# A transformer block on one core: a fifth Strassen pair, the odd gate product moved ahead of a change of pools, tiles shifted by 32 bytes

## The chip, the cores and the metric

The kernel runs on one NeuronCore of a Trainium2 chip. The metric is device time in microseconds (us) of one execution. TensorE (PE) multiplies matrices; VectorE (DVE) and ScalarE (ACT) work element by element; GpSimd (POOL) hardly works here; SyncE (SP) starts the DMAs. TensorE's stationary operand is loaded by a separate instruction, shown as PEld.

## The reference

One block on a sequence of 256 rows of 2048 numbers, float32:

```python
xn = rms_norm(h, norm1_g)
proj = xn @ w_in                        # u, v | q | c_kv | index q, k, w | gates
y_a = u * (W_s @ layer_norm(v) + b)     # chunk-causal spatial gating, gelu on u, v
y_b = sparse_attention(q, c_kv, ...)    # the top 64 keys of each query, by an indexer
mixed = g_a * (y_a @ w_oa) + g_b * (y_b @ w_ob)
h = h + mixed @ w_out
hn = rms_norm(h, norm2_g)
h = h + (silu(hn @ w_gate) * (hn @ w_up)) @ w_down      # w_gate, w_up: 2048 x 5632
out = rms_norm(h, final_g)
```

## The kernel before

Nearly all weights pass through the chip once. Each float32 operand is split in two, a high part rounded to float32r by ACT and the low rest by DVE (`split`, L70 to L78), and a product takes three matmuls: high by high, high by low, low by high (`mm3`, L88). The 256 rows make two tiles of 128, the 2048 columns four blocks of 512.

**Projections** (up to L494). Weights come in chunks of 128 x 1024 through the pool `wp` with four buffers each for the raw weights, their high and their low part (`wchunk`, L80). A natural group (`nat_group`, L93) has slices of x stationary and 512 weight columns moving. A transposed group (`tr_group`, L108; index queries, queries and keys) has 128 weight columns stationary and the 256 rows of x moving. The first projection (`kv`, L228 to L241) reads its chunk in two column halves of 296. The last of these stages is the output projection (L473), four blocks n; behind each come the residual add (L478), transposes on PE, and the operand for the feed-forward part. The feed-forward operand has 16 tiles of k, in eight pairs j. For j below `NS`, `s_operand` (L160) makes eight combinations of the pair's four 128 x 128 quarters for a Strassen product; for the others the tiles are only split.

**Feed-forward** (from L497). `pre.close()` gives up the pools of the projections, and `wq` and `fp` are laid over their bytes; a new tile waits for the old ones beneath it. A weight quad is 128 x 4 x 512, 1 MB, through three buffers (`quad`, `quad_split`). Eleven column blocks of 512 form five pairs, done by `s_group` (L520), and an odd one (`LB`), done by `plain_group`. An `s_group` makes 256 x 1024 of the gate or the up product. It goes over eight pairs j in `ORDER`. A Strassen pair (j below NS) takes DVE's three sums of weight quarters into `sums` (L534 to L536), a split of three raw quarters (1536 wide) and one of the four sums (2048 wide), and 7 products. A plain pair takes one split of 2048 and 8 products. The four Strassen sums m1, m5, m6, m7 lie in one PSUM pool of four banks (`aux`), the four results in the other (`acc`). After the last Strassen pair DVE combines the four into `u` (L549 to L553), after the last pair it evicts the results (L566 to L571).

PE's order is that of the program from L626 on (`manual_schedule`); the other engines' and everything before is ordered by Tile's scheduler. The order is: odd gate product, gate group 0, odd up product, up group 0, the odd block's down products, then for i = 1 to 4 gate group i, two down products of the pair before, up group i, two more. Beside the last half pair of a gate group PE transposes the block before for its down products (`beside`, L557); these transposes take `aux` banks.

Of the kernel before, what the change touches and what calls it, by code (L numbers as in the profile page):

```python
# [16 lines left out]
P = 128  # L17
# [13 lines left out]
KVW = LAT + IDXD + IDXH  # L31
NEG = -1.0e38
MARK = -3.0e38
NS = 4

A12, A22, A11, S1, S3, S2, S4, A21 = range(8)
WARM = 8
# [3 lines left out]
def block_kernel(ctx: ExitStack, tc: tile.TileContext, a, out):  # L41
# [4 lines left out]

    nc = tc.nc
    const = ctx.enter_context(tc.tile_pool(name="const", bufs=1))
    tp = ctx.enter_context(tc.tile_pool(name="tp", bufs=20))
    acc_p = ctx.enter_context(tc.tile_pool(name="acc", bufs=4, space=bass.MemoryType.PSUM))  # L50
    aux_p = ctx.enter_context(tc.tile_pool(name="aux", bufs=4, space=bass.MemoryType.PSUM))
    pre = ExitStack()
    np_ = pre.enter_context(tc.tile_pool(name="np", bufs=11))
    tq = pre.enter_context(tc.tile_pool(name="tq", bufs=4))
    wp = pre.enter_context(tc.tile_pool(name="wp", bufs=4))
    sp = pre.enter_context(tc.tile_pool(name="sp", bufs=1))
# [1 line left out]
    def t_tile(name, dt=F32R):  # L58
        return tp.tile([P, 4, T], dt, tag="T", name=name)
# [7 lines left out]
    def aux_tile(name):  # L67
        return aux_p.tile([P, 512], F32, tag="aux", name=name)
# [8 lines left out]
            nc.scalar.activation(h, src, AF.Copy, scale=scale)  # L77
            nc.vector.scalar_tensor_tensor(l, src, scale, hf, op0=ALU.mult, op1=ALU.subtract)  # L78

    def wchunk(src, cols):  # L80
        raw = wp.tile([P, 1024], F32, tag="raw", name="raw")
        h = wp.tile([P, 1024], F32R, tag="wh", name="wh")
        l = wp.tile([P, 1024], F32R, tag="wl", name="wl")
        nc.sync.dma_start(raw[:, :cols], src)
        split(h[:, :cols], l[:, :cols], raw[:, :cols])
        return h, l
# [21 lines left out]
    def tr_group(w, ks, x, name, bank=acc_tile, beside=None):  # L108


        acc = [bank(f"{name}_{b}").rearrange("p (c t) -> p c t", c=2) for b in range(2)]
        for c in range(len(ks) // 2):
            wh, wl = wchunk(w[c], 1024)
            for j in range(2):
                i = 2 * c + j
                xh, xl = x(ks[i])
                for ct in range(4):
                    s = slice(j * 512 + ct * P, j * 512 + (ct + 1) * P)
                    o = acc[ct // 2][:, ct % 2, :]
                    last = i == len(ks) - 1  # L120
                    nc.tensor.matmul(o, wh[:, s], xh, start=(i == 0 and ct % 2 == 0), stop=False,  # L121
                                     skip_group_check=True)
                    nc.tensor.matmul(o, wh[:, s], xl, start=False, stop=False, skip_group_check=True)  # L123
                    nc.tensor.matmul(o, wl[:, s], xh, start=False, stop=last, skip_group_check=True)  # L124
            if beside is not None:
                beside(c)
        return acc
# [345 lines left out]
    for n in range(4):  # L473
        hx = tp.tile([P, 2, 512], F32, tag="T", name=f"h{n}")
        nc.sync.dma_start(hx, x_nat[n])
        acc = nat_group(a["w_out"][n], KS, of(mx_t), f"out{n}")
        for t in range(2):
            nc.vector.tensor_tensor(hx[:, t], acc[t], hx[:, t], op=ALU.add)  # L478
        if 2 * n >= NS:
            h, l = t_tile(f"hh{n}"), t_tile(f"hl{n}")  # L480
            transposed(hx, f"h{n}", h, l, scale=g2[:, 4 * n:4 * n + 4])
            hT += [(z[0][:, s], z[1][:, s]) for z, s in (((h, l), slice(0, 2)), ((h, l), slice(2, 4)))]
        else:
            for b in range(2):
                k = 4 * n + 2 * b
                pt = aux_tile(f"h{n}_pt{b}").rearrange("p (c t) -> p c t", c=2)
                for c in range(2):
                    for t in range(2):
                        ct = 2 * b + c
                        nc.tensor.transpose(pt[:, c, t * P:(t + 1) * P], hx[:, t, ct * P:(ct + 1) * P], ident)  # L490
                hT.append(s_operand(pt, f"hS{k}", g2[:, k:k + 2]))
        sumsq(ss2, hx, n)
        hn.append(hx)
    r2 = row_rstd(ss2, "r2")  # L494


    pre.close()  # L497
    wq = ctx.enter_context(tc.tile_pool(name="wq", bufs=3, reuse_waits="tile"))
    fp = ctx.enter_context(tc.tile_pool(name="fp", bufs=1, reuse_waits="tile"))
# [11 lines left out]
        split(h, l, raw)  # L511
        return h, l

    def h_tile(k, t):

        return tuple(z[:, k % 2, t * P:(t + 1) * P] for z in hT[k // 2])

    ORDER = (0, 4, 1, 5, 2, 3, 6, 7)

    def s_group(w, name, beside=None):  # L520

        m1, m5, m7, m6 = (aux_tile(f"{name}_{z}") for z in ("m1", "m5", "m7", "m6"))
        c11, c12, c21, c22 = (acc_tile(f"{name}_{z}") for z in ("c11", "c12", "c21", "c22"))
        u = fp.tile([P, 4, 512], F32, tag="u", name=f"{name}_u")
        for n, j in enumerate(ORDER):
            first = n == 0
            if j < NS:  # L530
                raw = quad(w[j])
                tt = wq.tile([P, 4, 512], F32, tag="sums", name="sums", bufs=1)

                nc.vector.tensor_tensor(tt[:, 0:2], raw[:, 1:3], raw[:, 0:1].to_broadcast([P, 2, 512]), op=ALU.add)  # L534
                nc.vector.tensor_tensor(tt[:, 2], tt[:, 0], raw[:, 2], op=ALU.add)
                nc.vector.tensor_tensor(tt[:, 3], tt[:, 2], raw[:, 3], op=ALU.add)  # L536
                wh, wl = quad_split(raw[:, 1:4], 3)
                th, tl = quad_split(tt)
                xh, xl = hT[j]
                todo = [(m1, A11, wh, wl, 0), (c12, S4, wh, wl, 1), (c11, A12, wh, wl, 2),  # L540
                        (m5, S1, th, tl, 0), (m7, S3, th, tl, 1), (m6, S2, th, tl, 2), (c21, A22, th, tl, 3)]
                if first:
                    todo = [todo[z] for z in (0, 3, 4, 5, 6, 1, 2)]
                for o, s, h, l, i in todo:
                    mm3(o, xh[:, s], xl[:, s], h[:, i], l[:, i], first, j == NS - 1 and o in (m1, m5, m6, m7))
                if j == NS - 1:


                    nc.scalar.activation(u[:, 0], m1, AF.Copy)  # L549
                    nc.vector.tensor_tensor(u[:, 2], m6, u[:, 0], op=ALU.add)  # L550
                    nc.vector.tensor_tensor(u[:, 1], m7, u[:, 2], op=ALU.add)
                    nc.vector.tensor_tensor(u[:, 2], m5, u[:, 2], op=ALU.add)
                    nc.vector.tensor_tensor(u[:, 3], m5, u[:, 1], op=ALU.add)  # L553
            else:
                wh, wl = quad_split(quad(w[j]))
                for c in range(2):
                    if j == ORDER[-1] and c == 1 and beside is not None:  # L557
                        beside()
                    for t, i, o in ((0, 1, c11), (1, 1, c21), (0, 0, c12), (1, 0, c22)):

                        i = (i if c == 0 else (2, 3)[i])
                        xh, xl = h_tile(2 * j + c, t)
                        mm3(o, xh, xl, wh[:, i], wl[:, i], o is c22 and j == ORDER[1] and c == 0,
                            j == ORDER[-1] and c == 1)

        def f(t, j, dst=None):  # L566
            dst = u[:, 2 * j + t] if dst is None else dst
            if j == 0:
                nc.vector.tensor_tensor(dst, (c11, c21)[t], u[:, t], op=ALU.add)
            else:  # L570
                nc.vector.tensor_tensor(dst, (c12, c22)[t], u[:, 2 + t], op=ALU.subtract)  # L571
        return f, u
# [18 lines left out]
        at[b] = (h, l)  # L591

    def gate_blocks(i, beside):
        f, _ = s_group(a["w_fg"][i], f"fg{i}", beside)
        s = [f_tile(f"s{i}_{j}") for j in range(2)]
        for j in range(2):
            for t in range(2):
                f(t, j, s[j][:, t])
                nc.scalar.activation(s[j][:, t], s[j][:, t], AF.Silu, scale=r2[:, t:t + 1])
        return s  # L600
# [16 lines left out]
            nc.vector.scalar_tensor_tensor(hn[n][:, t], acc[t], r2[:, t:t + 1], hn[n][:, t],  # L617
                                           op0=ALU.mult, op1=ALU.add)

    def plain_x(k, t):  # L620
        if k < 2 * NS:
            return tuple(z[:, (A11, A12, A21, A22)[2 * t + k % 2]] for z in hT[k // 2])
        return h_tile(k, t)

    order = ctx.enter_context(ExitStack())
    order.enter_context(tc.manual_schedule(engines={mybir.EngineType.PE}))  # L626

    LB = NFB - 1

    def odd_gate():  # L630
        acc = plain_group([a["w_fg10"][c] for c in range(4)], plain_x, KT, f"fg{LB}")
        s = f_tile(f"s{LB}")
        for t in range(2):
            nc.scalar.activation(s[:, t], acc[t], AF.Silu, scale=r2[:, t:t + 1])
        return s

    def odd_up(s):
        acc = plain_group([a["w_fu10"][c] for c in range(4)], plain_x, KT, f"fu{LB}", aux_tile)
        for t in range(2):
            nc.vector.tensor_tensor(s[:, t], acc[t], s[:, t], op=ALU.mult)  # L640

    odd = odd_gate()
    for i in range(LB // 2):
        if i == 0:
            s = gate_blocks(0, None)
# [79 lines left out]
def _layout(np, i):  # L725
# [14 lines left out]
    def quads(w):  # L740
# [24 lines left out]
        "w_out": chunks(np.asarray(i["w_out"])[0]),  # L765
        "w_fg": strassen(np.asarray(i["w_ff_gate"])[0][:, :FF - 512]),
        "w_fu": strassen(np.asarray(i["w_ff_up"])[0][:, :FF - 512]),
        "w_fg10": quads(np.asarray(i["w_ff_gate"])[0][:, FF - 512:])[0],
        "w_fu10": quads(np.asarray(i["w_ff_up"])[0][:, FF - 512:])[0],
        "w_fd": quads(np.asarray(i["w_ff_down"])[0]),  # L770
        "final_g": np.asarray(i["final_g"]).reshape(2, 2, 512),
# [19 lines left out]
```

## Time and profile before

| | us |
|---|---|
| median of 3 runs (1607.43 to 1608.71) | 1608.19 |
| the profiled execution | 1608.13 |
| its span, first to last instruction | 1606.3 |
| PE busy | 1587.4, 99% |
| DVE busy | 1103.8, 69% |
| ACT busy | 778.1, 48% |
| 16 DMA queues' share | 55%, 191 GB/s |

A busy PE is one with a matmul in flight; matmuls overlap, so the pace is read from their starts. A wait is put down to what ended it. The chain that ended last is followed back from the last instruction.

### The profile page before, as it was taken

To read this page: it belongs to the slowest core of one execution; us is meant where nothing else is said; L and a number is where in the kernel's file an instruction comes from. 1 tells how busy PE (TensorE), PEld (TensorE's weight loads), DVE (VectorE), ACT (ScalarE), POOL (GpSimd) and SP (SyncE) were. 2 spreads that over 40 slices of the span, in tenths; PEclk is the share of its full clock that TensorE was granted. 3 is DMA by queue.
4 is the path that set the end of the run, shared out by engine and by line. 5 is a ranking of instruction groups with operands and counts; after the bars stand their busy time and mean duration, and the time that the engine had idled before them with its cause. 6 is when DMAs were issued, how large, how long until landed. Compare 5 with 4: busy or idle time off the path is not lost.

```text
span 1606.3 us, 19668 instructions
## 1 busy us (share of the span) xinstructions
PE 1587.4 (99%) x7834; PEld 1337.8 (83%) x7834; DVE 1103.8 (69%) x1216; ACT 778.1 (48%) x815; POOL 1.6 (0%) x8
## 2 busy tenths in 40 slices
PE   9999999999999999999999899999999999999997
PEld 8988989889778888888888688878888888888886
DVE  5695655565754444555564787888789778888785
ACT  6554454554544444444453654455445445446442
POOL 0000000000000000000000000000000000000000
PEclk9999999999999999999999999999999999999999
DMA  9646555545545555555665454555545555555561
GB/s 310 213 136 198 193 173 171 175 167 184 175 149 193 190 195 195 187 194 185 205 202 209 184 207 185 188 208 207 200 175 213 197 184 202 217 184 223 190 242 53
DMA packets 69115, 307.48 MB, mean 191 GB/s; under 512 B 8160, under 2 KB 8416, under 8 KB 52128
## 3 DMA queue, kind: packets, MB, share of 16 engines
q1 hardware_dynamic: 69024, 306.24, 55.3%
q8 instruction: 61, 1.00, 0.2%
q14 instruction: 30, 0.25, 0.0%
HBM read 304.11 MB, written 2.10 MB: 191 GB/s over the span
## 4 chain that ended last, share of the span: by engine, by line
PE 93%; DVE 4%; ACT 2%; issue 0%; DMA 0%; SPq 0%; ACTq 0%; DVEq 0%
PE fd L90 4%; PE fd L89 4%; PE fd L91 4%; PE g L89 4%; PE g L91 4%; PE g L90 4%; PE fu_c L90 3%; PE fu_c L91 3%; PE fu_c L89 3%; DVE wl L75 2%; PE fg_c L91 2%; PE fg_c L89 2%; PE fg_c L90 2%; PE q L124 2%; PE q L121 2%; PE q L123 2%
## 5 line engine op out<-in xcount | busy, mean ns | idle before, releaser
L75 DVE TENSOR_TENSOR wl<-raw,wh 128x1024 fp32r<-128x1024 f32 (+3 forms) x434 | 639.5, 1477 | 364.9 <-ACT wh L74 364.0
L74 ACT ACTIVATE wh<-raw 128x1024 fp32r<-128x1024 f32 (+3 forms) x434 | 545.4, 1262 | 541.7 <-PE g L91 86.0
L74 ACT ACTIVATE wh<-sums 128x2048 fp32r<-128x2048 f32 x40 | 76.7, 1917 | 172.5 <-DVE sums L536 141.4
L75 DVE TENSOR_TENSOR wl<-sums,wh 128x2048 fp32r<-128x2048 f32 x40 | 91.7, 2293 | 68.3 <-ACT wh L74 68.2
L89 PE MATMUL fd<-wh,ah 128*128 128x512 f32 x320 | 124.6, 389 | 0.0
L91 PE MATMUL fd<-wh,al 128*128 128x512 f32 x320 | 124.5, 389 | 0.0
L90 PE MATMUL fd<-wl,ah 128*128 128x512 f32 x320 | 124.5, 389 | 0.0
L91 PE MATMUL g<-wh,xl 128*128 128x512 f32 x256 | 100.9, 394 | 0.0
L89 PE MATMUL g<-wh,xh 128*128 128x512 f32 x256 | 100.8, 394 | 0.0
L90 PE MATMUL g<-wl,xh 128*128 128x512 f32 x256 | 99.9, 390 | 0.0
L124 PE MATMUL q<-xh,wl 128*128 128x256 f32 x256 | 72.5, 283 | 0.0
L121 PE MATMUL q<-xh,wh 128*128 128x256 f32 x256 | 72.5, 283 | 0.0
L123 PE MATMUL q<-xl,wh 128*128 128x256 f32 x256 | 72.4, 283 | 0.0
L89 PEld LDWEIGHTS fd<-wh,ah 128*128 128x128 f32 x320 | 60.1, 188 | 12.5
L91 PEld LDWEIGHTS fd<-wh,al 128*128 128x128 f32 x320 | 60.1, 188 | 12.5
L90 PEld LDWEIGHTS fd<-wl,ah 128*128 128x128 f32 x320 | 60.1, 188 | 12.4
L89 PE MATMUL fg_c<-wh,hh 128*128 128x512 f32 x160 | 62.6, 391 | 0.0
L89 PE MATMUL fu_c<-wh,hh 128*128 128x512 f32 x160 | 62.3, 390 | 0.0
L91 PE MATMUL fg_c<-wh,hl 128*128 128x512 f32 x160 | 62.3, 389 | 0.0
L90 PE MATMUL fg_c<-wl,hh 128*128 128x512 f32 x160 | 62.3, 389 | 0.0
L91 PE MATMUL fu_c<-wh,hl 128*128 128x512 f32 x160 | 62.2, 389 | 0.0
L90 PE MATMUL fu_c<-wl,hh 128*128 128x512 f32 x160 | 62.2, 389 | 0.0
(303 smaller groups left out, 3420.1 us busy)
## 6 DMA issues: line engine op xcount, KB each, us to landing
raw<-in_w_fg SPq DMA_DIRECT2D x44, 1024.0 KB, 4.8
raw<-in_w_fu SPq DMA_DIRECT2D x44, 1024.0 KB, 4.8
raw<-in_w_fd SPq DMA_DIRECT2D x44, 1024.0 KB, 4.7
raw<-in_w_z SPq DMA_DIRECT2D x64, 512.0 KB, 3.3
raw<-in_w_g SPq DMA_DIRECT2D x64, 512.0 KB, 3.2
raw<-in_w_q SPq DMA_DIRECT2D x32, 512.0 KB, 3.3
raw<-in_w_oa SPq DMA_DIRECT2D x32, 512.0 KB, 3.3
raw<-in_w_ob SPq DMA_DIRECT2D x32, 512.0 KB, 3.3
```

Source lines behind the costliest of these rows:

```text
L74: nc.scalar.activation(h, src, AF.Copy)
L75: nc.vector.tensor_tensor(l, src, hf, op=ALU.subtract)
L89: nc.tensor.matmul(o, lh, rh, start=start, stop=False, **kw)
L90: nc.tensor.matmul(o, lh, rl, start=False, stop=False, **kw)
L91: nc.tensor.matmul(o, ll, rh, start=False, stop=stop, **kw)
L121: nc.tensor.matmul(o, wh[:, s], xh, start=(i == 0 and ct % 2 == 0), stop=False, skip_group_check=True)
L123: nc.tensor.matmul(o, wh[:, s], xl, start=False, stop=False, skip_group_check=True)
L124: nc.tensor.matmul(o, wl[:, s], xh, start=False, stop=last, skip_group_check=True)
```

## The change

- `NS` goes from 4 to 5: pair 4, too, is a Strassen pair, in five gate and five up groups. `ORDER` becomes 0, 5, 1, 2, 6, 3, 4, 7. The output projection's block 2 now makes one Strassen operand and one plain pair, so that both kinds are made in one loop.
- The odd block's gate product leaves the feed-forward's manual order. It stands before `pre.close()`, with 1024-wide chunks through `wchunk` (eight of 512 KB instead of four of 1 MB), and `w_fg10` is laid out for that. Its Silu follows behind the new pools.
- The high and low weight tiles of `wp` get 64 columns more, and transposed groups use them from column 8 on, 32 bytes in.
- In `s_group` the split of the sums is made in two halves of 1024, each after the sums that it needs.
- The first gate group starts its first pair in the plain order (`free`), with the raw quarters' products ahead of the sums'.
- The pool `tp` has 21 tiles for 20, `np` 10 for 11, and the scratch area for descriptors is set to 1024 bytes.

```diff
-NS = 4
+NS = 5
...
-    tp = ctx.enter_context(tc.tile_pool(name="tp", bufs=20))
+    tp = ctx.enter_context(tc.tile_pool(name="tp", bufs=21))
...
-    np_ = pre.enter_context(tc.tile_pool(name="np", bufs=11))
+    np_ = pre.enter_context(tc.tile_pool(name="np", bufs=10))
...
-    def wchunk(src, cols):
+    def wchunk(src, cols, shift=0):
         raw = wp.tile([P, 1024], F32, tag="raw", name="raw")
-        h = wp.tile([P, 1024], F32R, tag="wh", name="wh")
-        l = wp.tile([P, 1024], F32R, tag="wl", name="wl")
+        h, l = (wp.tile([P, 1024 + 64], F32R, tag=z, name=z)[:, shift:shift + 1024] for z in ("wh", "wl"))
...
-            wh, wl = wchunk(w[c], 1024)
+            wh, wl = wchunk(w[c], 1024, 8)
...
-        if 2 * n >= NS:
-            h, l = t_tile(f"hh{n}"), t_tile(f"hl{n}")
-            transposed(hx, f"h{n}", h, l, scale=g2[:, 4 * n:4 * n + 4])
...
+        for b in range(2):
+            j, k = 2 * n + b, 4 * n + 2 * b
...
+            if j < NS:
+                hT.append(s_operand(pt, f"hS{j}", g2[:, k:k + 2]))
+            else:
+                hl = t_tile(f"hh{j}")
+                hT.append((hl[:, 0:2], hl[:, 2:4]))
                 for c in range(2):
...
+                    split(hl[:, c], hl[:, 2 + c], pt[:, c], scale=g2[:, k + c:k + c + 1])
...
+    LB = NFB - 1
+    odd_acc = [acc_tile(f"fg{LB}_{t}") for t in range(2)]
+    for c in range(KT // 2):
+        wh, wl = wchunk(a["w_fg10"][c], 1024)
+        for j in range(2):
+            k = 2 * c + j
+            for t in range(2):
+                xh, xl = plain_x(k, t)
+                mm3(odd_acc[t], xh, xl, wh[:, j * 512:(j + 1) * 512], wl[:, j * 512:(j + 1) * 512],
+                    k == 0, k == KT - 1)
     pre.close()
...
-    ORDER = (0, 4, 1, 5, 2, 3, 6, 7)
-
-    def s_group(w, name, beside=None):
+    odd = f_tile(f"s{LB}")
+    for t in range(2):
+        nc.scalar.activation(odd[:, t], odd_acc[t], AF.Silu, scale=r2[:, t:t + 1])
+
+    ORDER = (0, 5, 1, 2, 6, 3, 4, 7)
+
+    def s_group(w, name, beside=None, free=False):
...
-                th, tl = quad_split(tt)
+
+                th, tl = (wq.tile([P, 4, 512], F32R, tag=f"w{z}4", name=f"w{z}") for z in "hl")
+                for z in (slice(0, 2), slice(2, 4)):
+                    split(th[:, z], tl[:, z], tt[:, z])
...
-                if first:
+                if first and not free:
...
-        f, _ = s_group(a["w_fg"][i], f"fg{i}", beside)
+        f, _ = s_group(a["w_fg"][i], f"fg{i}", beside, i == 0)
...
-    odd = odd_gate()
...
-        "w_fg10": quads(np.asarray(i["w_ff_gate"])[0][:, FF - 512:])[0],
+        "w_fg10": chunks(np.asarray(i["w_ff_gate"])[0][:, FF - 512:])[0],
...
-    nc = bacc.Bacc("TRN2", target_bir_lowering=False, num_devices=1)
+    nc = bacc.Bacc("TRN2", target_bir_lowering=False, num_devices=1,
+                   dynamic_dma_scratch_size=1024)

```

## Rows read from the trace of the kernel before

**Rows 1.** Page, part 1: busy us, share of the span, instructions of each engine.

```profile
PE 1587.4 (99%) x7834; PEld 1337.8 (83%) x7834; DVE 1103.8 (69%) x1216; ACT 778.1 (48%) x815; POOL 1.6 (0%) x8
```

**Rows 2.** Sums by stage: length, busy PE, PEld, DVE, ACT, POOL; granted clock, DMA share, GB/s.

```profile
883.10:888.61 5.51, 1.48 (x9) 0.84 (x8) 4.22 (x18) 4.89 (x10) 0.00 (x0) 0.98 0.00 0
...
888.61:903.79 15.18, 13.53 (x48) 10.64 (x49) 10.06 (x6) 6.84 (x4) 0.00 (x0) 0.78 0.55 209
...
1040.69:1085.14 44.45, 42.86 (x198) 35.41 (x196) 36.93 (x31) 20.42 (x15) 0.00 (x0) 1.00 0.57 201
...
1169.46:1212.59 43.13, 42.88 (x198) 35.41 (x197) 35.44 (x30) 20.41 (x15) 0.00 (x0) 1.00 0.59 207
...
1234.35:1275.14 40.79, 40.79 (x181) 33.79 (x180) 31.32 (x25) 18.46 (x11) 0.00 (x0) 1.00 0.57 206
...
1169.46:1296.90 127.44, 127.19 (x569) 105.25 (x568) 106.96 (x87) 62.30 (x42) 0.00 (x0) 1.00 0.55 198
```

**Rows 3.** Timeline of PE: start, duration, instruction; first projection, index queries, output projection.

```profile
12.86 0.30 PE L89 MATMUL kv<-wh,xh 128*128 128x296 f32 x1
...
13.68 0.30 PE L89 MATMUL kv<-wh,xh 128*128 128x296 f32 x1
...
14.49 0.30 PE L89 MATMUL kv<-wh,xh 128*128 128x296 f32 x1
...
45.77 0.28 PE L121 MATMUL qi<-xh,wh 128*128 128x256 f32 x1
...
49.97 0.28 PE L124 MATMUL qi<-xh,wl 128*128 128x256 f32 x1
...
875.62 0.39 PE L89 MATMUL out<-wh,mxh 128*128 128x512 f32 x1
...
882.42 0.39 PE L89 MATMUL out<-wh,mxh 128*128 128x512 f32 x1
```

**Rows 4.** The chain that ended last: start, us, what; odd block, gate group.

```profile
888.71 2.30 DVE wl L75
...
891.84 0.43 PE fg L91
...
1208.27 1.75 PE a_pt L152 x16
```

**Rows 5.** Groups by line and shape, DVE and ACT: count, busy, mean ns, idle before.

```profile
L75 DVE TENSOR_TENSOR wl<-raw,wh 128x1024 fp32r<-128x1024 f32 x288 | 352.7, 1225 | 313.3 <-ACT wh L74 313.3
...
L75 DVE TENSOR_TENSOR wl<-sums,wh 128x2048 fp32r<-128x2048 f32 x40 | 91.7, 2293 | 68.3 <-ACT wh L74 68.2
...
L75 DVE TENSOR_TENSOR wl<-raw,wh 128x1536 fp32r<-128x1536 f32 x40 | 70.1, 1752 | 0.8 <-ACT wh L74 0.8
...
L534 DVE TENSOR_TENSOR sums<-raw 128x1024 f32<-128x1024 f32 x40 | 48.8, 1221 | 1.4 <-DMA raw<-in_w_fu 0.9
...
L535 DVE TENSOR_TENSOR sums<-sums,raw 128x512 f32<-128x512 f32 x40 | 27.5, 689 | 0.8
...
L74 ACT ACTIVATE wh<-raw 128x1024 fp32r<-128x1024 f32 x288 | 305.2, 1060 | 369.4 <-PE g L91 86.0 <-PE q L123 51.9 <-PE ob L91 50.8
...
L74 ACT ACTIVATE wh<-raw 128x2048 fp32r<-128x2048 f32 x90 | 171.8, 1912 | 125.1 <-PE fu_c L91 37.8 <-PE fg_c L91 32.4 <-PE fd L91 19.3
```

**Rows 6.** Timeline of DVE and PE in the gate group at 1296.90.

```profile
1296.80 1.41 DVE L617 SCALAR_TENSOR_TENSOR h<-fd,r_r,h 128x512 f32<-128x512 f32 x2
...
1302.86 2.29 DVE L75 TENSOR_TENSOR wl<-sums,wh 128x2048 fp32r<-128x2048 f32 x1 [2.06 <-ACT wh L74]
...
1322.39 2.29 DVE L75 TENSOR_TENSOR wl<-sums,wh 128x2048 fp32r<-128x2048 f32 x1 [2.06 <-ACT wh L74]
...
1324.11 0.39 PE L89 MATMUL fg_m<-wh,hS_h 128*128 128x512 f32 x1
...
1324.74 0.50 PE L90 MATMUL fg_m<-wl,hS_h 128*128 128x512 f32 x1 [0.24 <-DVE wl L75]
...
1326.98 0.69 DVE L550 TENSOR_TENSOR fg_u<-fg_m,fg_u 128x512 f32<-128x512 f32 x1
...
1333.19 0.68 DVE L553 TENSOR_TENSOR fg_u<-fg_m,fg_u 128x512 f32<-128x512 f32 x1
```

More of the change, by code (lines that the diff above doesn't have):

```diff
@@ L478, in block_kernel @@
             nc.vector.tensor_tensor(hx[:, t], acc[t], hx[:, t], op=ALU.add)
-        if 2 * n >= NS:
-            h, l = t_tile(f"hh{n}"), t_tile(f"hl{n}")
-            transposed(hx, f"h{n}", h, l, scale=g2[:, 4 * n:4 * n + 4])
[L482 to L486, printed above, removed]
+        for b in range(2):
+            j, k = 2 * n + b, 4 * n + 2 * b
+            pt = aux_tile(f"h{n}_pt{b}").rearrange("p (c t) -> p c t", c=2)
+            for c in range(2):
+                for t in range(2):
+                    ct = 2 * b + c
+                    nc.tensor.transpose(pt[:, c, t * P:(t + 1) * P], hx[:, t, ct * P:(ct + 1) * P], ident)
+            if j < NS:
[3 more added lines that the diff above has]
+                hT.append((hl[:, 0:2], hl[:, 2:4]))
                 for c in range(2):
[L488 to L491, printed above, removed]
+                    split(hl[:, c], hl[:, 2 + c], pt[:, c], scale=g2[:, k + c:k + c + 1])
         sumsq(ss2, hx, n)
@@ L494, in block_kernel, with h_tile, plain_x @@
     r2 = row_rstd(ss2, "r2")
+    def h_tile(k, t):
+        return tuple(z[:, k % 2, t * P:(t + 1) * P] for z in hT[k // 2])
+    def plain_x(k, t):
+        if k < 2 * NS:
+            return tuple(z[:, (A11, A12, A21, A22)[2 * t + k % 2]] for z in hT[k // 2])
+        return h_tile(k, t)
+    LB = NFB - 1
[8 more added lines that the diff above has]
+                    k == 0, k == KT - 1)
     pre.close()
@@ L512, in quad_split @@
         return h, l
-    def h_tile(k, t):
-        return tuple(z[:, k % 2, t * P:(t + 1) * P] for z in hT[k // 2])
-    ORDER = (0, 4, 1, 5, 2, 3, 6, 7)
-    def s_group(w, name, beside=None):
+    odd = f_tile(f"s{LB}")
+    for t in range(2):
+        nc.scalar.activation(odd[:, t], odd_acc[t], AF.Silu, scale=r2[:, t:t + 1])
+    ORDER = (0, 5, 1, 2, 6, 3, 4, 7)
+    def s_group(w, name, beside=None, free=False):
         m1, m5, m7, m6 = (aux_tile(f"{name}_{z}") for z in ("m1", "m5", "m7", "m6"))
@@ L618, in down_one @@
                                            op0=ALU.mult, op1=ALU.add)
[L620 to L623, printed above, removed]
     order = ctx.enter_context(ExitStack())
     order.enter_context(tc.manual_schedule(engines={mybir.EngineType.PE}))
[L628 to L635, printed above, removed]
     def odd_up(s):
```

## Prediction

> **What bounds the kernel now.** I read the page first, then sums by stage, then the chain that ended last, then single instructions. TensorE (PE) is busy 99% of the span and every other engine less [rows 1]. So time can only come from fewer or faster matmuls, or from the few places where PE waits. To see the second kind I cut the span into stages [rows 2]. In the stretch from the last output-projection matmul to the first gate matmul (883.10 to 888.61) PE has almost no work, in the next one (888.61 to 903.79) it runs at a granted clock of 0.78, and in the gate groups of the feed-forward part it loses between 0.25 and 1.6 us; the up groups and the down products lose nothing. The same rows show what is close behind: in one full turn of the feed-forward loop (1169.46 to 1296.90) VectorE (DVE) works 107.0 of 127.4 us, 84%. That is the reserve which a fifth Strassen pair draws on.
>
> The pace of a matmul comes from starts far apart in one row of equal work [rows 3]. With 512 columns, 30 matmuls start between 875.62 and 882.42: 226.7 ns each. With 256 columns, 35 between 45.77 and 49.97: 120 ns each. Their difference, 106.7 ns for 256 columns, leaves 13.3 ns that belong to the matmul and not to its columns.
>
> **Part 1, the fifth Strassen pair.** A Strassen pair costs PE 7 products of 3 matmuls, a plain pair 8 of 3. One pair is converted in each of five gate and five up groups: 10 x 3 x 226.7 ns = **-6.8 us**, all of it on PE and so on the path.
>
> **Part 2, the odd block's gate product in front of the pool change.** Before, PE goes from 883.10 to 903.79, 20.7 us, for 48 matmuls (10.9 us) and eight transposes (0.9 us by sixteen in 1.75 [rows 4]): 8.9 us are lost. The chain shows why: the residual add, the transposes and their splits, then a split of a whole 2048-wide weight block whose low part runs 2.30 us from 888.71 [rows 4], and after that wait ten matmuls that take 0.43 us each, nearly twice the 0.227 of a full clock [rows 2 to 4]. After the change the first 72 of the 96 odd matmuls (rows 0 to 11 of k) need nothing from the last output block. They are 16.3 us of PE work to lie beside that chain, with 1024-wide splits (1.06 and 1.23 us, [rows 5]) already streaming through the pool that fed the projections. I take 8.4 back and leave 0.5. The bounds are 0 and 8.9. The price of no cover, if the scheduler puts the odd matmuls behind the chain, is the whole 8.9. What is late next is the first gate group: its high and low sums tiles reuse bytes of the weight chunks, so they wait for the end of the odd product. Raw, sums and the three-quarter tiles lie on bytes that are free earlier, and the order with the sums' products behind (free) gives the low half 2 us (nine matmuls) against 1.23.
>
> **Part 3, DVE and ScalarE (ACT) in the feed-forward groups.** On DVE a Strassen pair costs sums 1.22 + 0.69 + 0.69, the three-quarter low part 1.75, the low part of the sums 2.29 [rows 5], together 6.64; in halves the last is 2 x 1.23, so 6.80. A plain pair costs 2.29. PE takes 4.76 and 5.44 us for them. So every converted pair moves 4.5 us onto DVE: the loop's turn rises from 107.0 to 107.0 + 2 x 4.5 + 8 x 0.16 = 117.3 of some 125.8 us, 93%. It still fits, on average; what matters is the stretch inside a gate group. There, from the group's first matmul to the second half of the last Strassen pair's sums, PE has 4 x 21 + 2 x 24 + 15 = 147 matmuls, 33.3 us. DVE must meanwhile do two evictions (1.41, [rows 6]), the second pair's sums and low part (5.05), three whole pairs (20.4) and a plain one (2.29): 29.2 us. So 4.1 us are left for waits. In the kernel before, each low part of the sums waits 2.0 us for ACT's high part, and the last of them makes PE wait [rows 6]. The halves are to remove that: ACT's first half (1.06) lies beside the other two sums (1.38), its second beside the first low half (1.23). When ACT is in another split (1.9 us) a wait of about 1 remains, and the scheduler may put the last plain pair's 2.29 ahead. That gives 29.2 to 29.2 + 4 + 2.3 = 35.5 against 33.3: a stall between 0 and 2.2 us.
>
> A second place is behind the last Strassen pair. Before, two plain pairs (10.9 us) followed it; now one (5.4 us). In that time the four sums of the products must leave PSUM, since the transposes beside the last half pair take the same four banks. In the trace these four short operations take from 1326.98 to 1333.87, 6.9 us, because 2.28 us splits get between them [rows 6]. PE would reach the transposes 2.7 us after the last Strassen product, so up to 4.2 us of wait; nothing if the splits are no longer ready by then. For both places I take 2.0 us in each of four gate groups (bounds 0 and 6.4), 1.5 in the first (no down product before it gives a lead; bounds 0 and 2.2), none in up groups, where DVE works 4 us less [rows 2]: **+9.5**, bounds 0 and 28. Against that stand the gate groups' old waits, which this replaces: 1.9 in the group at 1040.69 (1.6 of PE idle [rows 2], and the restart) and 0.55 in each of three others (a start 0.63 us after the one before instead of 0.23, and a little behind it, [rows 6]): **-3.5**.
>
> **Part 4, the shift by 32 bytes.** It concerns 1344 matmuls of the transposed groups (256 columns), so that a nanosecond each is 1.34 us. By the sizes of the pools every tile that they read starts 32 bytes past a multiple of 64; the stationary weights move to a multiple of 64, the moving tiles stay. No row shows a displaced stationary operand. The nearest ones show a displaced moving one: the first projection's second column half starts 1184 bytes in, 32 off from 64. Its six matmuls take 13.68 to 14.49, those of the undisplaced half 12.86 to 13.68 [rows 3]: 0.81 and 0.82 us. By that row the shift does nothing, to within 1.7 ns each, 2.2 us. The other end is that the 13.3 ns per matmul are a collision of the two reads and vanish: 1344 x 13.3 = 17.9 us. I take **0**, the nearer row, with bounds of -17.9 and +2.2.
> The Trainium skill, "TensorE: Matmul & The Clock Gate" (Step-by-step: what each phase is for), says that TensorE reads stationary and moving operands through two independent ports, so that loading the next weights takes no bandwidth from the running matmul. That speaks against any effect of the shift; the rows with 13.3 ns per matmul neither prove nor exclude it.
>
> **Edits at nothing.** Four 1 MB loads become eight of 512 KB: DMA is 0.55 to 0.59 busy where weights stream [rows 2]. The one more pair's operand needs a 1024-wide split (1.06 and 1.23 us, [rows 5]) and a few short operations of ACT and DVE, beside the last output block's 96 matmuls, 21.8 us. One tile less in one pool and one more in another, and the smaller scratch area, change no instruction.
>
> **Sum.** The profiled execution took 1608.13 us, span 1606.3 and 1.8 around it; the median of three runs is 1608.19, the same. 1608.1 - 6.8 - 8.4 - 3.5 + 9.5 + 0 = **1598.9**. Its own range is 1592 (new stalls near 2) to 1607 (near 18).
>
> **Rivals.**
> *The shift pays.* If the 13.3 ns are a collision, some or all of 17.9 us goes: 1581 to 1595, at half 1590. For it: the same 13.3 at 256 and at 512 columns looks like a fixed number of lost reads. Against it: the equal halves of the first projection. The Trainium skill, "TensorE: Matmul & The Clock Gate" (Wait — 56ns, not 53.3ns?), puts the fixed part of a warm matmul at about 2.5 ns; as an estimate from that page the shift could give at most 1344 x 10.8 ns = 14.5 us, 1584.
> *DVE becomes the bound; slower.* If the halves don't shorten the wait because ACT, in order, is busy with other splits, a pair costs DVE 6.8 + 2.06, the gate stretch 29.2 + 4 x 2.06 = 37.4 us against 33.3, 4.1 us lost, and likewise in every one of ten groups: 1608.1 - 18.7 + 41 = 1630. It decides from 18.7 / 10, 1.9 us per group. For it: 93% of a turn; against it: the high halves fit beside the sums.
> *The gap moves.* The odd product covers nothing, or the first gate group waits as long as the odd product did: 8.4 us lost again, 1607.3, no change that can be told.
>
> **Chances.** Forecast 0.50, shift pays 0.27, slower 0.13, gap moves 0.10. The likeliest gives 1599. For 8 in 10 the range takes in five sixths of the shift's 17.9 us, 15, and the moved gap: 1584 to 1608; left out are the slower case and the shift's far end. A difference of 0.2% (3.2 us) is about what a measurement can tell. Faster: 0.45 of the forecast's 0.50, 0.27, 0.02 of the gap's: 0.74. Slower: 0.13 and 0.01: 0.14. The rest, 0.12, is no change.
>
> **What would show it.** Right: 96 odd matmuls follow the output projection 0.227 us apart with the transposes among them at a full clock; 7804 matmuls; no DVE wait of 2 us before a low half; gate groups with 1 to 3 us of PE idle. The shift is told by the transposed groups' starts: 0.120 us apart or less. Wrong: PE waiting in up groups, a gap that stands between the odd product and the first gate group, or transposes that wait for PSUM by more than 4 us.

## The result and the profile after

The changed kernel takes **1598.51 us** (median of 4 runs, 1598.35 to 1599.92), the kernel before 1608.24 beside it (4 runs, 1607.43 to 1608.71): a ratio of 0.9941, with a 95% interval from 0.9929 to 0.9954. The forecast was 1598.9, faster. The profiled span is 1596.8 us for 1606.3, so 9.5 us are to be found in the trace. The total is right; its parts are not, and the rest of this document is about that.

The page of the kernel after: part 1 (busy us, share, instructions), and from part 5 the low parts of the sums (out<-in, count | busy, mean ns | idle before).

```profile
PE 1577.3 (99%) x7804; PEld 1329.3 (83%) x7804; DVE 1151.6 (72%) x1312; ACT 803.1 (50%) x880; POOL 1.6 (0%) x8
...
L75 DVE TENSOR_TENSOR wl<-sums,wh 128x1024 fp32r<-128x1024 f32 x100 | 120.5, 1219 | 11.8 <-ACT wh L74 11.8
```

30 matmuls fewer than in [rows 1], 47.8 us more work for DVE, and DVE's idle time before a low part of the sums is 11.8 us in 100 instructions, where [rows 5] had 68.3 in 40. The halves do what they were made for.

The sums by stage (length, busy PE, PEld, DVE, ACT, POOL; granted clock, DMA share, GB/s): the odd block's gate product; the entry into the first gate group; gate groups 1 and 2.

```profile
880.70:902.97 22.27, 22.27 (x103) 18.35 (x102) 12.48 (x26) 9.23 (x15) 0.00 (x0) 1.00 0.50 189
903.22:911.30 8.08, 4.64 (x14) 3.13 (x13) 5.56 (x4) 7.55 (x7) 0.00 (x0) 0.82 0.23 80
...
1037.64:1085.00 47.36, 45.59 (x208) 37.47 (x207) 44.55 (x44) 25.46 (x23) 0.00 (x0) 1.00 0.57 200
1165.48:1208.00 42.52, 42.52 (x197) 35.44 (x196) 39.91 (x39) 22.91 (x21) 0.00 (x0) 1.00 0.61 215
```

The first row is the forecast's picture: PE without a break at a full clock. The second is what the forecast had not: a gap of the old kind [rows 2], only later. Gate group 1 loses 1.8 us of PE, gate group 2 nothing at all, though DVE is busy for 39.9 of its 42.5 us.

PE at that gap (start, us, instruction, [idle before <- what ended it]):

```profile
880.47 0.39 PE L90 MATMUL out<-wh,mxl 128*128 128x512 f32 x1
...
903.22 0.39 PE L90 MATMUL fg<-wh,hh 128*128 128x512 f32 x1
905.76 0.51 PE L88 MATMUL fg_m<-wh,hS_h 128*128 128x512 f32 x1 [2.15 <-ACT wh L74]
907.55 0.50 PE L89 MATMUL fg_m<-wl,hS_h 128*128 128x512 f32 x1 [1.29 <-DVE wl L75]
...
908.74 0.63 PE L90 MATMUL fg_c<-wh,hS_l 128*128 128x512 f32 x1
909.16 0.63 PE L88 MATMUL fg_c<-wh,hS_h 128*128 128x512 f32 x1
...
913.89 0.39 PE L88 MATMUL fg_c<-wh,hh 128*128 128x512 f32 x1
```

From the last odd matmul (903.22) to 913.89 there are 22 starts. At 226.7 ns they need 5.0 us; they took 10.7. So **5.7 us** are lost, in two waits and then in matmuls 0.42 us apart, at half the clock (granted 0.50 from 908.60 to 911.60, the level of 1.2 GHz). Before, the entry lost 8.9.

ACT over the same time shows why:

```profile
893.85 1.28 ACT L537 ACT_TABLE_LOAD   x1
902.97 1.37 ACT L537 ACTIVATE s<-fg,r_r 128x512 f32<-128x512 f32 x2 [7.84 <-PE fg L90]
904.23 1.47 ACT L74 ACTIVATE wh<-raw 128x1536 fp32r<-128x1536 f32 x1
```

ACT works in its own order. It has loaded the table for the odd block's Silu and then stands for 7.84 us at that Silu, which needs the end of the odd product. The first gate group's high part (904.23) is behind it, and PE waits for that.

Now the whole. The last output-projection matmul starts at 880.47, 2.4 us earlier than before. From there to the last matmul of all it is 707.22 us for 714.47 before, -7.25: the 6.8 of the 30 matmuls, and 0.45 of waits. What all waits of PE cost behind the projections has hardly moved (some 12 us in both kernels); they stand in other places.

### The profile page after: what moved, and what is told of

It reads as the page before. It is cut to its first block, busy times and chain, and to the rows that moved or that the text cites. A ratio compares the mean times of both kernels' runs of the same rounds, so it can differ in the third digit from the quotient of the medians.

```text
span 1596.8 us, 19798 instructions
## 1 busy us (share of the span) xinstructions
PE 1577.3 (99%) x7804; PEld 1329.3 (83%) x7804; DVE 1151.6 (72%) x1312; ACT 803.1 (50%) x880; POOL 1.6 (0%) x8
## 4 chain that ended last, share of the span: by engine, by line
PE 95%; DVE 2%; ACT 1%; issue 1%; DMA 0%; SPq 0%; ACTq 0%; DVEq 0%
PE fd L88 5%; PE fd L90 5%; PE fd L89 5%; PE g L89 4%; PE g L90 4%; PE g L88 4%; PE fu_c L88 3%; PE fu_c L89 3%; PE fu_c L90 3%; PE fg_c L88 2%; PE fg_c L89 2%; PE fg_c L90 2%; PE q L122 2%; PE q L123 2%; PE q L120 2%; PE u L90 2%
## 5 line engine op out<-in xcount | busy, mean ns | idle before, releaser
L74 ACT ACTIVATE wh<-sums 128x1024 fp32r<-128x1024 f32 x100 | 104.0, 1055 | 147.9 <-DVE sums L555 47.5
L75 DVE TENSOR_TENSOR wl<-sums,wh 128x1024 fp32r<-128x1024 f32 x100 | 120.5, 1219 | 11.8 <-ACT wh L74 11.8
L90 PEld LDWEIGHTS fd<-wh,al 128*128 128x128 f32 x320 | 60.1, 188 | 12.5
L89 PEld LDWEIGHTS fd<-wl,ah 128*128 128x128 f32 x320 | 60.1, 188 | 12.5
L555 DVE TENSOR_TENSOR sums<-raw 128x1024 f32<-128x1024 f32 x50 | 61.1, 1221 | 3.4 <-DMA raw<-in_w_fu 2.6
L88 PEld LDWEIGHTS g<-wh,xh 128*128 128x128 f32 x256 | 48.1, 188 | 10.8 <-issue 1.0
L89 PEld LDWEIGHTS g<-wl,xh 128*128 128x128 f32 x256 | 48.1, 188 | 10.2 <-issue 0.5
L90 PEld LDWEIGHTS g<-wh,xl 128*128 128x128 f32 x256 | 48.1, 188 | 10.1 <-issue 0.5
L88 PE MATMUL u<-wh,xh 128*128 128x512 f32 x128 | 51.7, 404 | 0.0
L90 PE MATMUL u<-wh,xl 128*128 128x512 f32 x128 | 50.8, 397 | 0.0
```

What stands on the lines that cost most here:

```text
L74: nc.scalar.activation(h, src, AF.Copy)
L75: nc.vector.tensor_tensor(l, src, hf, op=ALU.subtract)
L88: nc.tensor.matmul(o, lh, rh, start=start, stop=False, **kw)
L89: nc.tensor.matmul(o, lh, rl, start=False, stop=False, **kw)
L90: nc.tensor.matmul(o, ll, rh, start=False, stop=stop, **kw)
```

## Experiments

The times of the kernel before, run beside these, are 1607.93 to 1608.36.

**1. The shift taken out.** The tiles keep their 64 spare columns.

```diff
-            wh, wl = wchunk(w[c], 1024, 8)
+            wh, wl = wchunk(w[c], 1024)
```

> The changed kernel with the transposed groups' tiles back at column 0; the tiles keep their 64 spare columns. Theory (the offset itself shortens a matmul): the starts of 256-column matmuls go back from 118.33 to 119.96 ns, and the 1344 of them cost 2.2 us, 1600.7. Rival (the wider spacing of the tiles, 4352 bytes instead of 4096, does it): the pace stays at 118.3 and the time at 1598.5.

Measured: 1601.69 us, ratio 0.9959 (0.9945 to 0.9974). Two starts of the index queries' matmuls in the kernel after, then in this one:

```profile
46.64 0.28 PE L123 MATMUL qi<-xh,wl 128*128 128x256 f32 x1
...
48.06 0.28 PE L123 MATMUL qi<-xh,wl 128*128 128x256 f32 x1
```

```profile
46.63 0.28 PE L122 MATMUL qi<-xl,wh 128*128 128x256 f32 x1
...
47.71 0.28 PE L122 MATMUL qi<-xl,wh 128*128 128x256 f32 x1
```

12 steps in 1.42 us are 118.3 ns; 9 steps in 1.08 us are 120.0, the pace of before [rows 3]. So the offset itself pays, not the wider spacing of the tiles: 1.63 ns by 1344 matmuls is 2.2 us. The median moved by 3.2; in the profiled executions 0.55 us of that lies ahead of the first transposed group, and some 0.5 in a stop inside it.

**2. Five pairs without the halves.**

```diff
-                for z in (slice(0, 2), slice(2, 4)):
-                    split(th[:, z], tl[:, z], tt[:, z])
+                split(th, tl, tt)
```

> The changed kernel with the sums split whole (2048 wide) again, five Strassen pairs kept. Theory of the prediction (the halves carry the fifth pair): VectorE waits 2 us for ScalarE in every Strassen pair again, a gate group's stretch needs some 37 us for 33 us of matmuls, so 3 to 5 us are lost in most of ten groups: 1625 to 1645. Rival (the buffers are ahead enough, the halves matter little): within 3 us of 1598.5.

Measured: 1632.11 us, ratio 1.0142 (1.0125 to 1.0159): slower than before. What PE waited for (total, times, longest), then DVE and PE at the last Strassen pair of gate group 2:

```profile
PE fg_m L89 <- DVE wl L75: 16.1, 13, 1.8
PE a_pt L151 <- DVE fg_u L576: 6.5, 4, 1.9
```

```profile
1211.62 2.29 DVE L75 TENSOR_TENSOR wl<-sums,wh 128x2048 fp32r<-128x2048 f32 x1 [2.06 <-ACT wh L74]
```

```profile
1213.97 0.50 PE L89 MATMUL fg_m<-wl,hS_h 128*128 128x512 f32 x1 [1.82 <-DVE wl L75]
```

This is the forecast's slower rival, built on purpose: it priced this at 1630. Its place is narrower than the rival said, though: all waits are in gate groups, none in up groups. Against the matmuls' pace gate groups 1 to 4 lose 7.0 to 7.7 us each and gate group 0 some 10, where the rival had 4.1 in each of ten groups; that its total comes near is luck. Waits are not the whole loss: behind that of 1.82 us the granted clock is 0.50 from 1214.90 to 1217.80, and eight matmuls start 0.43 us apart. The fifth pair pays only with the halves; they are worth 33.6 us here.

**3. The Silu written later in the program,** behind the first pair's splits.

```diff
-    for t in range(2):
-        nc.scalar.activation(odd[:, t], odd_acc[t], AF.Silu, scale=r2[:, t:t + 1])
...
+                if first and free:
+                    odd_silu()
+                    c21, c22 = (acc_tile(f"{name}_{z}") for z in ("c21", "c22"))
```

> The changed kernel with the odd block's Silu issued behind the first gate pair's splits instead of ahead of them (the last two result banks are taken after it). Theory (ScalarE, in order, sits on the Silu's wait for the odd product while the first gate split is ready behind it): the wait of 2.15 + 1.29 us at 903.2 and the slow clock after it go, 5.4 us, and the two later waits of 1.9 us in the first gate group shrink: 1590 to 1593.5. Rival (the split waits for the bytes of the old pools, which come free at the end of the odd product): less than 1.5 us gained.

Measured: 1599.01 us, ratio 0.9944 (0.9929 to 0.9959). ACT:

```profile
902.76 1.37 ACT L539 ACTIVATE s<-fg,r_r 128x512 f32<-128x512 f32 x2 [7.84 <-PE fg L90]
904.02 1.47 ACT L74 ACTIVATE wh<-raw 128x1536 fp32r<-128x1536 f32 x1
```

The edit didn't make the case that was to be tested: the scheduler put the Silu ahead of the split again, with the same 7.84 us. It says nothing on the reason; experiment 5 does.

**4. The odd product back behind the pool change,** with the old order in the first group. All else as in the change.

```diff
-    odd_acc = [acc_tile(f"fg{LB}_{t}") for t in range(2)]
-    for c in range(KT // 2):
-        wh, wl = wchunk(a["w_fg10"][c], 1024)
...
     pre.close()
...
-        f, _ = s_group(a["w_fg"][i], f"fg{i}", beside, i == 0)
+        f, _ = s_group(a["w_fg"][i], f"fg{i}", beside)
...
+    odd = odd_gate()
```

> The changed kernel with the odd block's gate product back behind the change of pools, 1 MB quads, and the first gate group in its old order; five pairs, halves and the shift kept. Theory (the move took back part of the entry gap, 8.9 us before, 5.4 left after, and gave the first gate group two waits of 1.9 us): 0 to 4 us slower, 1598.5 to 1602.5, with the entry gap as before and no waits in the first gate group. Rival (the move is worth its predicted 8.4 us): 1607.

Measured: 1598.59 us, ratio 0.9940 (0.9925 to 0.9955). PE at the old place of the gap:

```profile
886.34 0.80 PE L88 MATMUL fg<-wh,hS_h 128*128 128x512 f32 x1 [3.69 <-ACT wh L74]
888.78 0.80 PE L89 MATMUL fg<-wl,hS_h 128*128 128x512 f32 x1 [1.64 <-DVE wl L75]
```

The old gap is back: from 880.83 to 902.10 for 48 matmuls and eight transposes, which is 9.5 us lost by the measure that gave 8.9 before. The first gate group's two waits are gone. The sum is the same as with the move. **As it was made, the move is worth nothing**: it takes 8.9 us from one place and puts 5.7 behind the odd product and 3.8 into the first gate group.

**5. ACT's order forced.** The splits of the first Strassen pair and of the first plain pair are issued ahead of the odd block's Silu.

```diff
+                if first and free:
+                    p5 = tuple(wq.tile([P, 4, 512], F32R, tag=f"w{z}4", name=f"w{z}") for z in "hl")
+                    raw5 = quad(w[ORDER[1]])
+                    with tc.issue_after(ins(hi)):
+                        hi = split(*p5, raw5)
+                    with tc.issue_after(ins(hi)):
+                        odd_silu()
+                    c21, c22 = (acc_tile(f"{name}_{z}") for z in ("c21", "c22"))
```

> The changed kernel with ScalarE's order forced: the first gate pair's three splits and the first plain pair's split are issued ahead of the odd block's Silu. The late Silu of the run before was put back in front by the scheduler, so ScalarE still waited 7.8 us on it. Theory (that order is the entry gap): PE goes from the odd product to the first gate group without a wait and at the full clock, 5.4 us gained, and the first gate group's two waits of 1.9 us shrink by what VectorE gets done earlier: 1589.5 to 1593.5. Rival (the split waits for bytes of the old pools or for VectorE): a wait of over 2 us stays at the same place, 1597 or more.

Measured: **1593.72 us**, ratio 0.9908 (0.9893 to 0.9922). ACT, then PE:

```profile
896.56 1.06 ACT L74 ACTIVATE wh<-sums 128x1024 fp32r<-128x1024 f32 x1 [1.11 <-DVE sums L560]
...
903.89 1.93 ACT L74 ACTIVATE wh<-raw 128x2048 fp32r<-128x2048 f32 x1 [3.33 <-PE fg L91]
907.13 1.27 ACT L540 ACTIVATE s<-fg,r_r 128x512 f32<-128x512 f32 x2
```

```profile
903.46 0.39 PE L91 MATMUL fg<-wh,hh 128*128 128x512 f32 x1
903.69 0.39 PE L89 MATMUL fg_m<-wh,hS_h 128*128 128x512 f32 x1
...
909.84 0.50 PE L90 MATMUL fg_c<-wl,hh 128*128 128x512 f32 x1 [0.77 <-DVE wl L75]
```

The first gate matmul follows the last odd one after 0.23 us. The wait on ACT's order was the gap: 4.8 us by the medians, 5.2 by the start of the last matmul (1582.53 for 1587.69). The move is worth about 5 us, once nothing stands at the head of ACT's queue. The other half of the theory failed: the first gate group's waits didn't shrink. They cost 3.8 us over the pace, as in the kernel after, now in three waits (at 908.67, 923.35 and 939.24), and the time lies just above the range. So the Silu's place doesn't explain these waits.

**6. Four pairs with everything else kept.**

```diff
-NS = 5
+NS = 4
...
-    ORDER = (0, 5, 1, 2, 6, 3, 4, 7)
+    ORDER = (0, 4, 1, 5, 2, 3, 6, 7)
```

> The changed kernel with four Strassen pairs and the old order of pairs; the odd product's place, the halves and the shift kept. Theory (the fifth pair saves 30 matmuls and its price in waits is small): 6.8 us more of matmuls, less the waits that the fifth pair brought in the gate groups (3.8 in the first, 2.2 in the second), 1600 to 1605. Rival (the fifth pair's waits eat its gain): 1598.5 or less.

Measured: 1600.17 us, ratio 0.9948 (0.9931 to 0.9964). PE, its only long waits behind the projections:

```profile
907.13 0.72 PE L88 MATMUL fg_m<-wh,hS_h 128*128 128x512 f32 x1 [2.15 <-ACT wh L74]
908.92 0.79 PE L89 MATMUL fg_m<-wl,hS_h 128*128 128x512 f32 x1 [1.07 <-DVE wl L75]
```

The entry loses 6.4 us; no gate group has any wait. So with the halves, and without a fifth pair, the old 3.5 us are gone (no run has the halves without the odd product's move as well), and the gate groups' 6.1 us in the kernel after (1.87 + 1.89 + 0.55 + 1.77) come with the fifth pair. Of its 6.8 us some 1.4 are left: 6.8 - 6.1 + 0.7 (6.4 at the entry for 5.7). The medians say 1.7, a difference that their intervals don't separate from nothing.

**7 and 8. Other distances: 64 and 16 bytes.** One execution each.

```diff
-            wh, wl = wchunk(w[c], 1024, 8)
+            wh, wl = wchunk(w[c], 1024, 16)     # 64 bytes; in experiment 8: 4, 16 bytes
```

> The changed kernel with the transposed groups' tiles shifted by 64 bytes instead of 32. Theory (what counts is where the stationary weights stand to a multiple of 64 bytes, which 32 changes and 64 does not): 256-column matmuls start 120.0 ns apart, 2.2 us slower. Rival (any displacement against the moving tile does it): 118.3 ns.

> The changed kernel with the transposed groups' tiles shifted by 16 bytes instead of 32. Theory (only a start at a multiple of 64 bytes helps): 120 ns between starts of 256-column matmuls, 2.2 us slower, or more than 120 if a start off 32 costs more lines. Rival (half of 32 gives half of the gain): 119.1 ns.

Measured: 1594.38 us with 64 bytes, 1599.91 with 16. Starts of index queries and of keys with 64 bytes:

```profile
46.55 0.28 PE L122 MATMUL qi<-xl,wh 128*128 128x256 f32 x1
...
48.02 0.28 PE L123 MATMUL qi<-xh,wl 128*128 128x256 f32 x1
...
199.76 0.28 PE L123 MATMUL k<-cT_h,wl 128*128 128x256 f32 x1
...
201.17 0.28 PE L123 MATMUL k<-cT_h,wl 128*128 128x256 f32 x1
```

13 steps in 1.47 us, 113.1 ns, and 12 in 1.41, 117.5: over whole groups 113.3 or 117.8, and here each group holds one of the two. With 16 bytes every group runs at 118.3, as with 32. That distance counts modulo 64, my theory then, is wrong; that 32 is as good as any is wrong too.

**9 and 10. Longer distances, and the natural groups.** Experiment 5's order; transposed groups at 128 and 192 bytes; the natural groups' weights, which are their moving operand, at 64 and 128. One execution each.

```diff
-            wh, wl = wchunk(w[c], 1024)          # nat_group
+            wh, wl = wchunk(w[c], 1024, 16)      # experiment 10: 32
...
-            wh, wl = wchunk(w[c], 1024, 8)       # tr_group
+            wh, wl = wchunk(w[c], 1024, 32)      # experiment 10: 48
```

> The kernel with the splits ahead of the odd Silu, the transposed groups' tiles shifted by 128 bytes, and those of the natural groups (weights moving, 512 columns) by 64 bytes. The shifts of 0, 16, 32 and 64 bytes gave 120.0, 118.3, 118.3 and 113.3 or 117.8 ns by group between starts. Theory (the gain grows with the distance up to some period): transposed 113.3 ns or less. Rival (64 was a lucky phase, multiples of 128 are as 0): 120 ns. Natural groups: 226.7 ns if only the stationary side counts; some 6 ns less if the distance between the two tiles counts, whichever moves, which would be 6 us and more for their 2300 matmuls.

> As the run before, with the transposed groups' tiles shifted by 192 bytes and the natural groups' by 128. Theory (period of 128 bytes): 192 is as 64, 113.3 or 117.8 ns. Rival (the gain grows on): less than 113. Natural groups: 226.7 ns if only the stationary side counts.

Measured: 1598.74 and 1606.19 us, 5.0 and 12.5 more than experiment 5. The transposed groups run at 118.7 ns with 128 bytes, the first of them at 120.0, and at 113.3 or 117.8 with 192, as with 64. The natural groups, at 226.67 ns undisplaced, run at 228.9 with 64 bytes and at 232.3 to 233.3 with 128, a loss that neither reading had. So a distance helps where 128 weight columns are stationary and 256 rows move, and harms where 512 columns move.

**11. The best of both.** Experiment 5's order, transposed groups at 64 bytes.

> The kernel with the splits ahead of the odd Silu and the transposed groups' tiles shifted by 64 bytes; natural groups unshifted. Theory (both gains stand in different stages and add): 1593.7 less what 114.5 to 115.6 instead of 118.3 ns gives 1344 matmuls, 4 to 5 us: 1588.5 to 1590. By group the pace is 113.3 or 117.8 ns; were all groups in the slow one, 1593.

Measured: **1590.88 us** (1590.56 to 1591.3), ratio 0.9891 (0.9877 to 0.9906), faster than both kernels. Mean pace of the queries 115.6 ns, of the index queries 116.4, of the keys 115.6: against 118.33 that is 2.1 + 0.7 + 0.5 = 3.3 us, and 2.8 were measured against experiment 5. That is less than the 4 to 5 us expected: more of the work ran at the slow pace than in experiment 7, at the same distance. The first group of index queries even changed its pace:

```profile
42.82 0.28 PE L123 MATMUL qi<-xl,wh 128*128 128x256 f32 x1
...
46.90 0.28 PE L123 MATMUL qi<-xl,wh 128*128 128x256 f32 x1
...
47.60 0.28 PE L123 MATMUL qi<-xl,wh 128*128 128x256 f32 x1
...
54.66 0.28 PE L123 MATMUL qi<-xl,wh 128*128 128x256 f32 x1
```

36 steps in 4.08 us are 113.3 ns; behind a start that came late (0.36 us after the one at 46.90), 60 steps in 7.06 us are 117.7. So one group, with its offset unchanged, can have either pace.

**12. The stationary side of the natural groups displaced.** Experiment 11, with the activations' tiles moved by 64 bytes and the transposed groups' weights by 128, so that those keep their 64.

```diff
+    def big(pool, dt, name, n):
+        return pool.tile([P, 1024 + 128], dt, tag="T", name=name)[:, 16:1040].rearrange("p (a b) -> p a b", a=n)
...
-        return tp.tile([P, 4, T], dt, tag="T", name=name)
+        return big(tp, dt, name, 4)
...
-            wh, wl = wchunk(w[c], 1024, 8)
+            wh, wl = wchunk(w[c], 1024, 32)
```

> As the run before, with every tile of the large pool (the stationary operands of the natural groups and of the feed-forward part, the moving ones of the transposed groups) displaced by 64 bytes, and the transposed groups' weights by 128, so that there the stationary side stays 64 ahead. Theory (a stationary operand 64 bytes ahead of the moving one saves 6.7 ns, whatever the group): 512-column matmuls start about 220 ns apart, some 5500 of them save 37 us: 1552. Rival (only 256-column matmuls, whose weight loads fill their whole time, gain; at 512 the pace is 226.7 at equal start and longer at any other, as for displaced moving tiles): 226.7 to 233 ns, 1589 to 1625.

Measured: 1620.80 us, ratio 1.0075 (1.0058 to 1.0092). PE in an up group:

```profile
1399.65 0.39 PE L94 MATMUL fu_c<-wh,hS_l 128*128 128x512 f32 x1
...
1401.28 0.39 PE L92 MATMUL fu_m<-wh,hS_h 128*128 128x512 f32 x1
```

7 steps in 1.63 us: 233 ns for 226.7. The rival was right; the natural groups lose either way. The transposed ones keep 113.4 to 114.5 on the mean, so for them it is the distance that counts, not which side is moved. The pitch of these tiles changed along with the offset (4608 bytes for 4096). The last down products of this run tell the two apart. All have a displaced stationary tile. In the first lines the moving tiles (`kept_h`, `kept_l`) come from the displaced pool too; in the last lines they don't, and are 256 columns wide:

```profile
1591.18 0.39 PE L93 MATMUL last<-kept_l,ah 128*128 128x512 f32 x1
...
1594.58 0.39 PE L93 MATMUL last<-kept_l,ah 128*128 128x512 f32 x1
...
1598.41 0.28 PE L94 MATMUL last<-wh,al 128*128 128x256 f32 x1
...
1600.45 0.28 PE L94 MATMUL last<-wh,al 128*128 128x256 f32 x1
```

15 steps in 3.40 us are 226.7 ns: with both sides displaced nothing is lost, so neither the offset nor the pitch does the harm, but the distance. 18 steps in 2.04 us are 113.3 ns, for 120.0 in experiment 11. So with activations stationary, too, 64 bytes help 256 columns and harm 512: what matters is the width, not which operand holds the weights.

## Why the prediction was right, and where it was not

The forecast's terms beside what the trace and the experiments gave:

| part | forecast | measured |
|---|---|---|
| 1, 30 matmuls fewer | -6.8 | -6.8 |
| 2, the entry: 8.9 before | -8.4 (0.5 left) | -3.2 (5.7 left) |
| 3, old waits of the gate groups | -3.5 | -3.5 |
| 3, new waits, gate group 0 | +1.5 | +3.8 |
| 3, new waits, gate groups 1 to 4 | +8.0 | +2.3 |
| 4, the shift | 0 | -2.2 |
| sum | -9.2 | -9.6 (span: -9.5) |

**Part 1** holds: 7804 matmuls at an unchanged 226.7 ns.

**Part 2 is the step that failed.** Its first half holds: the odd matmuls follow the output projection 0.227 us apart, with the transposes among them. Its second half asked what is late next and looked for bytes of the old pool and for the order of the products. It didn't ask what is queued ahead of the first split on ACT. The diff shows it: the odd block's Silu stands between the odd product and the first gate group, it needs the product's last matmul, and it shares an in-order engine with the splits. ACT stood 7.84 us, with DVE behind it. Experiment 5 shows that this, and not the reuse of bytes, was the gap. The rival "the gap moves" foresaw that a wait would come back at the first gate group, and its 8.4 us come out as 5.2 over the forecast at the entry and 2.3 in the first gate group; together 7.5. The Silu accounts for the first of these alone. Its total, 1607.3, didn't come, because two other terms missed the other way.

**Part 3, the new waits,** was mis-sized in both directions. Four gate groups were to wait 2.0 us each; gate group 1 waits 2.3, the other three nothing. The bound from below was 0, and I took 2.0 out of caution. The end of the gate stretch shows how near it is. DVE's four short operations (L574 to L577) in gate group 1, then in gate group 2; below them PE's transposes in the same two groups:

```profile
1073.68 0.68 DVE L574 TENSOR_TENSOR fg_u<-fg_m,fg_u 128x512 f32<-128x512 f32 x1
1074.40 0.69 DVE L575 TENSOR_TENSOR fg_u<-fg_m,fg_u 128x512 f32<-128x512 f32 x1
1075.04 2.29 DVE L75 TENSOR_TENSOR wl<-raw,wh 128x2048 fp32r<-128x2048 f32 x1
1077.25 0.68 DVE L576 TENSOR_TENSOR fg_u<-fg_m,fg_u 128x512 f32<-128x512 f32 x1
...
1199.81 0.68 DVE L574 TENSOR_TENSOR fg_u<-fg_m,fg_u 128x512 f32<-128x512 f32 x1
1201.86 0.68 DVE L577 TENSOR_TENSOR fg_u<-fg_m,fg_u 128x512 f32<-128x512 f32 x1
```

```profile
1078.58 0.66 PE L151 MATMUL a_pt<-ident,s 128*128 128x128 f32 x4 [1.50 <-DVE fg_u L577]
...
1202.89 1.91 PE L151 MATMUL a_pt<-ident,s 128*128 128x128 f32 x16
```

In gate group 1 a split of 2.29 us gets between the four short operations, and the last transposes wait 1.50 us for their bank: the forecast's second place, with the mechanism that it named. In gate group 2 the four run in one piece and end at 1202.5, before PE asks at 1202.89. The first place is as close: the low part of the last sums' second half is due at the 149th start of the group, 33.5 us in. In gate group 1 its low part ends 33.9 us in, in gate group 2 32.1 (1196.38 + 1.22 - 1165.48); the forecast's two ends were 29.2 and 35.5. So DVE comes 0.4 us late there, which costs 0.55, or 1.4 us early, which costs nothing. At the second place the price is a step: nothing, or 1.77 us, as a long split gets in between or not. Why gate group 2 comes with more lead than gate group 1 was not tested. Gate group 0, for which the forecast saw no lead, waits twice (1.87 and 1.89 us), more than its bound of 2.2; in experiment 4, with the odd product behind the pool change, it doesn't. With the Silu out of the way (experiment 5) the 3.8 us stay, so their cause is open; what the runs show is that they come with the move (the new order of the first pair included, which experiment 4 also took back) and the fifth pair together, since experiment 6, with four pairs, hasn't got them.

**Part 4** took 0 from the nearest row, a displaced moving operand in the first projection. Its own margin was 1.7 ns for each matmul; the effect is 1.63, so that row could not have shown it. The rival "the shift pays" is what happened, at its small end.

**The total** is right because the misses cancel: +5.2 at the entry, +2.3 in gate group 0, -5.7 in gate groups 1 to 4, -2.2 by the shift, -0.4 in all.

## What to carry to other kernels

When work is moved ahead to cover a gap, look at each in-order engine for what else is queued there: a Silu that needs the moved work's end was worth 4.8 us while it stood ahead of the next stage's first split, and nothing behind it. A second engine that is 90% busy against the first costs not a little everywhere but nothing or a couple of microseconds, as a long operation gets in front of a short one or not; so size such a term by counting the groups that have no lead. And check a total by its parts: this one was right to 0.4 us with four terms off by 2 to 6.

## What the runs showed of the hardware

The part of a matmul's time that doesn't belong to its columns depends on the distance in bytes between the stationary and the moving tile in a partition. The distance is the difference of the offsets that the kernels give to the tiles; addresses are not in the traces. Pace in ns, of whole groups:

| distance, bytes | 256 columns moving | 512 columns moving |
|---|---|---|
| 0 | 120.0 | 226.7 |
| 16 | 118.3 | not tried |
| 32 | 118.3 | not tried |
| 64 | 113.3 or 117.8 | 228.9 (moving side displaced), 233.3 (stationary side) |
| 128 | 118.7, one group 120.0 | 232.3 to 233.3 (moving side) |
| 192 | 113.3 or 117.8 | not tried |

With 256 columns 64 and 192 bytes alike, and 128 nearly as 0, look like a period of 128. With 512 columns the distances harm, and no such period shows: 128 bytes cost more than 64 on the same side. Why equal offsets give two paces, with a change inside a group in experiment 11, and why the two widths differ in sign, stays open. The Trainium skill, "TensorE: Matmul & The Clock Gate" (Step-by-step: what each phase is for), has stationary and moving operands on independent ports, so that loading weights takes nothing from the running matmul. These paces don't agree with that: with the same columns and loads, the distance alone moves a matmul by up to 6.7 ns, which it could not if the two reads never met. Where they meet, no run shows. The fixed part of about 2.5 ns that the Trainium skill gives on the same page (Wait — 56ns, not 53.3ns?) was not reached either; at the best pace here, 113.3 ns, 6.6 ns are left over the columns' 106.7.
